# A hybrid decoder layer on one core: output weights centred by accumulating DMAs, two gate pairs ahead of the embedding, pooling operands begun one group earlier

## The chip, the cores and the metric

The kernel runs on one core of one Trainium2 chip. The metric is the time of the program on the device in microseconds (us), the median of three runs; lower is better. Engines are named as in the profile: PE (TensorE matmuls), PEld (its weight loads), DVE (VectorE), ACT (ScalarE), POOL (GpSimd), SP (the queue that issues most DMAs).

## The reference, cut to what matters

One layer on x of 1024 tokens by 2048 channels, all in float32:

```
h = x @ w_in + b_in                                   # 2048 -> 4352 columns
q, k, v, g_attn, u_pool, g_pool = split(h)
a = banded_sink_attention(q, k, v) * silu(g_attn)     # 16 heads of 64, window 128
b = multiscale_pool(u_pool, w_pool) * silu(g_pool)    # trailing means over 2/4/8/16, 4 groups
mix = concat([a, b]) @ w_out
ple = sigmoid(x @ w_gate_ple) * (p @ w_ple)
out = layer_norm(2**0.25 * x + mix + ple, gain, bias)
```

The layer norm subtracts the mean over the 2048 output channels. The kernel gets a part of that subtraction by centring rows of `w_out` beforehand: from each row of its first half (1024 input channels) the mean over the 2048 output columns is subtracted.

## The kernel before, in words

**Work on PE.** All large matmuls are cut into *jobs*: two blocks of 128 output columns by 1024 input channels by 1024 tokens. A job is done as seven block products in place of eight (a Strassen-like scheme, orders `ALONE` and `BESIDE`, lines 46 to 48). Each product is 12 matmuls of 128x128 by 128x512: weights and operands are split into a high and a low fp32r part, and three of the four combinations are multiplied (`mm3`, lines 176 to 181). A weight block is loaded as `raw`, combined on DVE (lines 215 to 218) and split by ACT into `wh` and by DVE into `wl` (`make_unit`), four products ahead of PE. Results are gathered from PSUM into `part` by ACT (`copy`) and DVE (`add`), line 346 and line 122.

**Order.** Jobs run in *groups*: a group is one job (7 products) or a pair (14 products). After each product a clock of *ticks* advances (`tick`), and work beside the matmuls is registered at a tick: `after(n, fn)` runs `fn` n ticks on; `later(n, fn)` does the same, and in addition queues what `fn` issues on PE, ACT and DVE behind the product work last marked on that engine. Instructions of SP and POOL get no such place from `later`. The order of each engine's queue is then made by the planner of the language, which takes the recorded order as priority and starts an instruction on an idle engine once its operands and buffers are free in its own estimate of time. Every queue runs strictly in that order on the chip.

**Stages** (`run`, lines 884 to 910). Five jobs of k, v, q for the first half of the input channels (s1); 25 jobs of s2: k, v, q for the second half, and everything else for the first; 20 jobs of s3: gates `gp`, pool inputs `u`, attention gates `ga` and the embedding gate `wgate` for the other half, with what follows them; s4 and s5: the output projection; s6: its last 256 tokens; the norm. The list `rest` (line 855) sets the order in s2 and s3: gp0, u0, gp1, u1, gp2, u2, gp3, u3, ga0, wgate 0 to 7, ga1, ga2, ga3. The first two and the last two jobs of a stage form pairs.

**Beside s2.** Attention runs as 16 half-heads, nine ticks apart (`heads`, called from lines 995 and 996): `begin` fetches the queries and the bias, `split` splits the queries (ACT and DVE, tick 3), `score` multiplies on PE and adds bias on DVE (tick 4 and on), `shift`, `softmax` (with an add on POOL), `share`, `trans` (PE transposes, four `affine_select` on POOL each, line 551), `value`. In the same stage `centre_weights` (line 709, called at line 999) reads the first half of `w_out` twice, in 32 cells of 256 KB each time, through the one buffer `cw`: the first pass adds up rows on DVE (line 722), the second subtracts the mean on DVE (line 122, by `tt`) and stores the cell to `wc` in DRAM.

**Beside s3.** `pool_u` makes the trailing sums of a pool block; after two blocks `mix` multiplies by `w_pool` (tick 10 after `pool_u`) and multiplies by the stored gate `sgp`, which is fetched at tick 8. `embed_in` fetches and splits p, `embed_w` the columns of `w_ple`; `embed` adds `ple` and x to each finished wgate block. They use 16 buffers `s` (`slots`) and six buffers `e` (`extras`). At the last pair of s3 these pools are closed and the same memory holds six `slots1` and eight `twos1` buffers (lines 1019 to 1024); into the latter `pooled()` fetches the pooling half of the concatenation `cc` by DMAs that ACT's queue issues (line 267). `make_pooled` splits these into the operands of s4 (`split_unit`, ACT and DVE, and four pairs of subtractions on DVE): its first two steps run at the start of the first group of s4, the next ones every two ticks. `gate_ahead` fetches the attention result `pre` for the gates.

Of the kernel before, what the change touches and what calls it, by code (L numbers as in the profile page):

```python
# [24 lines left out]
F32 = mybir.dt.float32  # L25
F32R = mybir.dt.float32r
AF = mybir.ActivationFunctionType
ALU = mybir.AluOpType
# [3 lines left out]
P = 128  # L32
T = 512
H = 4 * P
D = 2048
NB = 16
# [27 lines left out]
class Layer:  # L64
# [405 lines left out]
    def heads(self, h, j):  # L470
        nc, g = self.nc, j // 4
# [108 lines left out]
        self.later(3, split)  # L580
        for bq in range(4):
            t = 4 * (bq // 2)
            self.after(4 + 2 * bq, lambda bq=bq: score(bq))
            if bq % 2:
                self.after(8 + t, lambda bq=bq: shift(bq - 1))
                self.after(14 + t, lambda bq=bq: trans(bq - 1))
            self.after(9 + t, lambda bq=bq: softmax(bq))
            self.later(11 + t, lambda bq=bq: share(bq))
            self.after(19 + t + bq % 2, lambda bq=bq: value(bq))


    def gate_ahead(self, j):
# [15 lines left out]
    def pool_u(self, j, c):  # L608
        nc, g = self.nc, j // 2
        w = 2 << g  # L610
        out = []
        for h in range(2):
            u = self.slot()
            if h == 0:
                nc.gpsimd.memset(u[:, 0:16], 0.0)
            else:
                self.ident_act(u[:, 0:16], c[:, 0, T - 16 :], self.c(C_BIN + U0 + j))
            self.ident_act(u[:, 16:], c[:, h], self.c(C_BIN + U0 + j))
            cur, d, first = u, 1, 1
            while d < w:  # L620
                nxt = self.slot()
                end = 2 * d == w
                f = 16 if end else first
                self.tt(nxt[:, f:], cur[:, f:], cur[:, f - d : T + 16 - d], ALU.add)
                cur, d = nxt, 2 * d
                first = first + d
            if h == 0:
                self.tt(cur[:, 16 : 16 + 16], cur[:, 16 : 16 + 16], self.c(C_HEAD + 16 * g, 16), ALU.mult, nc.gpsimd)
            nc.vector.scalar_tensor_tensor(out=cur[:, 16:], in0=cur[:, 16:], scalar=1.0 / w, in1=u[:, 16:],
                                           op0=ALU.mult, op1=ALU.subtract)  # L630
            out.append(self.split(cur[:, 16:], 2 * (j % 2) + h < 3))
        self.diff[j] = out
        if j % 2:
            f = slice((g % 2) * T, (g % 2) * T + T)
            self.after(4, lambda: self.got.update({("wp", g): self.fetch(self.wpool[g // 2][:, f])}))
            self.later(8, lambda: self.got.update({("wp", g): self.split(self.got["wp", g])}))
            self.after(8, lambda: self.got.update({("sg", g): [[self.fetch(self.sgp[2 * g + e][:, h * T : h * T + T]) for e in range(2)] for h in range(2)]}))
            self.later(10, lambda: self.mix(g))

    def mix(self, g):  # L640
# [67 lines left out]

    def centre_weights(self, at, by):

        nc = self.nc
        cells = [(b, h) for b in range(NB) for h in range(2)]
        sums = self.fix.tile([P, 8, NB], F32, name="wsum")
        mean = self.fix.tile([P, 8], F32, name="wmean")
        now = []

        def fetch(b, h):
            now.append(self.load(self.tile(self.cw, [P, H], "cw"), self.wout[b, 0][:, h * H : h * H + H]))

        def add_up(b, h):  # L720
            k = now.pop().rearrange("p (k m) -> p k m", k=4)
            nc.vector.reduce_sum(sums[:, 4 * h : 4 * h + 4, b : b + 1], k, axis=mybir.AxisListType.X)

        def take_mean():
            nc.vector.reduce_sum(mean.rearrange("p (k b) -> p k b", b=1), sums, axis=mybir.AxisListType.X)
            nc.vector.tensor_scalar(out=mean, in0=mean, scalar1=1.0 / D, scalar2=None, op0=ALU.mult)

        def centre(b, h):
            w = now.pop()
            k = w.rearrange("p (k m) -> p k m", k=4)  # L730
            m = mean[:, 4 * h : 4 * h + 4].rearrange("p (k m) -> p k m", m=1).broadcast_to([P, 4, P])
            self.tt(k, k, m, ALU.subtract)
            self.load(self.wc[b, 0][:, h * H : h * H + H], w)

        for step in (add_up, centre):
            for c in cells:
                self.after(at, lambda c=c: fetch(*c))
                self.later(at + 2, lambda c=c, step=step: step(*c))
                at += by if step is centre and c[0] % 3 else 2
            if step is add_up:  # L740
                self.later(at + 1, take_mean)
                at += 2

    def mean_to_subtract(self, total, w, cut):

# [78 lines left out]
    def run(self):  # L824
# [27 lines left out]
        store = lambda w: hid if w is win else gat  # L852
        qkv = [(win, *p) for p in [(KB, VB)] + pairs(Q0, 4)]
        ga, gp, u = ([(win, *p) for p in pairs(b, 4)] for b in (GA0, GP0, U0))
        rest = [j for two in zip(gp, u) for j in two] + ga[:1] + [(wgate, *p) for p in pairs(0, 8)] + ga[1:]

        def keep(where):
            return lambda b, c: self.load(where[b], flat(c))
# [134 lines left out]
        self.after(5, lambda: build_kv(KB, self.k_build, 0))  # L993
        self.after(6, lambda: build_kv(VB, self.v_build, 0))
        for i in range(16):
            self.after(t - 1 + 9 * i, lambda i=i: self.heads(i % 2, i // 2))
        self.after(t + 63 + 8, lambda: build_kv(KB, self.k_build, 1))
        self.after(t + 63 + 22, lambda: build_kv(VB, self.v_build, 1))
        self.centre_weights(8, 3)
        begin, *steps = self.set_kept(xs[0], kept)  # L1000
        for i in range(1, n2):
            if i == n2 - 1:
# [6 lines left out]
        for i in range(n3):  # L1009
            if i == 1:  # L1010
                over.close()
                over = ExitStack()
                self.extras = self.work_pool("e2", 6, over)
            if self.groups[g + i + 1][0][0].b[0] == 0 and i < n3 - 1:
                self.after(1, self.embed_in)
                self.after(4, lambda: self.embed_w(0))
            if i == n3 - 1:

                over.close()
                work.close()  # L1020
                work = ExitStack()
                self.slot_n = T
                self.slots = self.work_pool("slots1", 6, work)
                self.twos = self.work_pool("twos1", 8, work)
                pooled()
                for n, b in enumerate(b for j in s3[-2:] for b in j.b):
                    self.after(4 + n, lambda b=b: self.gate_ahead(b - GA0))
            self.run_group(g + i, () if i else steps)
        g += n3

# [33 lines left out]
        for i in range(n4):  # L1064
            if i == 1:
                work.close()
                work = ExitStack()
                self.twos = self.work_pool("twos2", 8, work)
                p6.extend(5 * [pp] + [self.work_pool("p6", 1, work)])
                d0 = self.work_pool("d0", 4, work)  # L1070
            if i == n4 - 2:
                attended()
            self.run_group(g + i, () if i else make_pooled, renew if i == n4 - 1 else None)
        g += n4


# [134 lines left out]
```

## Time and profile before

| | |
|---|---|
| Median of 3 runs | 1505.13 us (1503.91 to 1507.74) |
| Profiled execution, its own time | 1504.51 us |
| Its span in the profile | 1502.8 us |
| Granted TensorE clock, mean | 0.99 |
| Busy: PE, DVE, ACT, POOL | 97%, 75%, 52%, 19% of the span |
| DMA: moved, mean rate | 280.38 MB, 187 GB/s |

A busy share is the time in which an instruction of that engine was in flight, over the span. Matmuls overlap each other, so PE at 97% is not a statement on its peak; what counts is where PE has no matmul in flight, and the spacing of the matmuls. Stretches of the trace are named by us from the span's start. The stages begin at these times, read as the first matmul of their first product: s2's first pair 110.8, its single jobs 148.9, its last pair 632.4; s3's first pair 676.6, single jobs 717.9, last pair 1105.3; s4's first pair 1146.8, single jobs 1190.7; s5 1305.0.

### The profile page before, as it was taken

The page shows a single profiled execution, that of the slowest core. Times are in us where ns is not written, and L with a number is a line of the kernel's source. Part 1 is how long each engine was busy: PE and PEld are TensorE (multiplying, and loading weights), DVE is VectorE, ACT ScalarE, POOL GpSimd, SP SyncE. Part 2 cuts the span into 40 slices and gives each one's busy share as a digit, 9 for nine tenths or more (in the row PEclk, how much of TensorE's full clock was granted, in tenths as well). Part 3 has the DMA queues.
Part 4 walks back from the last instruction along what each step waited for, and adds up shares of the span by engine and source line. Part 5 has one row for each costly group of instructions (what it writes and reads, how often), then busy time and mean ns, then how long its engine had stood idle before and what let it go on. Part 6 is the DMA issues. An engine that isn't in the chain of part 4 may idle for free. (4 is left out here: it accounts for less than half of the span.)

```text
span 1502.8 us, 20461 instructions
## 1 busy us (share of the span) xinstructions
PE 1453.8 (97%) x6972; PEld 1225.5 (82%) x6972; DVE 1119.7 (75%) x2030; ACT 781.1 (52%) x1550; POOL 278.9 (19%) x388
## 2 busy tenths in 40 slices
PE   8999999999999999999999998999998999999986
PEld 6788888888878888888887786888886888899985
DVE  7788678888787877888675695556558866987785
ACT  5464566666666656566633353333337433555484
POOL 0000123332333332231111111000001111111241
PEclk9999999999999999999999999999999999999998
DMA  7563875445445555557766667575768678586564
GB/s 262 202 218 101 250 208 178 140 167 174 166 168 176 174 193 180 172 182 245 189 158 175 180 155 240 160 207 160 206 189 270 150 193 236 140 239 134 153 230 143
DMA packets 101721, 280.38 MB, mean 187 GB/s; under 512 B 11632, under 2 KB 16880, under 8 KB 101616
## 3 DMA queue, kind: packets, MB, share of 16 engines
q1 hardware_dynamic: 76400, 199.89, 39.9%
q0 software_dynamic: 19712, 67.64, 19.6%
q10 hardware_dynamic: 5504, 11.54, 2.3%
q8 instruction: 55, 0.90, 0.2%
q14 instruction: 50, 0.41, 0.1%
HBM read 193.04 MB, written 85.98 MB: 186 GB/s over the span
## 5 line engine op out<-in xcount | busy, mean ns | idle before, releaser
L222 ACT CAST wh<-raw 128x512 fp32r<-128x512 f32 x428 | 264.1, 620 | 450.8 <-PE qa L180 143.2
L122 DVE TENSOR_TENSOR wl<-raw,wh 128x512 fp32r<-128x512 f32 x428 | 298.2, 702 | 141.4 <-ACT wh L222 138.5
L346 ACT COPY part<-qa 128x512 f32<-128x512 f32 (+1 forms) x180 | 103.9, 577 | 54.0 <-PE qa L181 53.0
L551 POOL TENSOR_SCALAR_AFFINE_SELECT s<-s 128x512 fp32r<-128x512 f32 x128 | 101.0, 801 | 150.5 <-ACT s L544 101.1
L122 DVE TENSOR_TENSOR part<-part,qb 128x512 f32<-128x512 f32 (+1 forms) x120 | 81.0, 675 | 50.5 <-PE qb L181 47.0
L179 PE MATMUL qa<-b11h,wh 128*128 128x512 f32 (+2 forms) x292 | 110.7, 380 | 2.0 <-ACT b11h L248 1.7
L180 PE MATMUL qa<-b11l,wh 128*128 128x512 f32 (+2 forms) x292 | 109.5, 375 | 0.2 <-DVE b11l L122 0.2
L181 PE MATMUL qa<-b11h,wl 128*128 128x512 f32 (+2 forms) x292 | 109.0, 374 | 0.4 <-DVE wl L122 0.4
L179 PE MATMUL qb<-b21h,wh 128*128 128x512 f32 (+2 forms) x292 | 109.3, 374 | 0.0
L181 PE MATMUL qb<-b21h,wl 128*128 128x512 f32 (+2 forms) x292 | 108.9, 373 | 0.0
L180 PE MATMUL qb<-b21l,wh 128*128 128x512 f32 (+2 forms) x292 | 108.7, 372 | 0.0
L179 PE MATMUL qb<-t1h,wh 128*128 128x512 f32 (+1 forms) x260 | 102.1, 393 | 4.3 <-DVE part L122 2.9
L179 PE MATMUL qa<-t2h,wh 128*128 128x512 f32 (+1 forms) x260 | 100.6, 388 | 3.5 <-ACT wh L222 3.5
L179 PE MATMUL qa<-t3h,wh 128*128 128x512 f32 (+1 forms) x260 | 100.9, 388 | 3.1 <-ACT part L346 3.1
L181 PE MATMUL qb<-t1h,wl 128*128 128x512 f32 (+1 forms) x260 | 101.1, 389 | 1.5 <-DVE wl L122 1.5
L181 PE MATMUL qa<-t2h,wl 128*128 128x512 f32 (+1 forms) x260 | 100.0, 385 | 1.5 <-DVE wl L122 1.5
L180 PE MATMUL qb<-t1l,wh 128*128 128x512 f32 (+1 forms) x260 | 100.9, 388 | 0.0
L179 PE MATMUL qa<-t4h,wh 128*128 128x512 f32 (+1 forms) x260 | 100.4, 386 | 0.3 <-DVE part L122 0.3
L179 PE MATMUL qb<-b22h,wh 128*128 128x512 f32 (+1 forms) x260 | 100.4, 386 | 0.0
L180 PE MATMUL qa<-t4l,wh 128*128 128x512 f32 (+1 forms) x260 | 99.7, 383 | 0.0
L181 PE MATMUL qa<-t4h,wl 128*128 128x512 f32 (+1 forms) x260 | 99.7, 383 | 0.0
L180 PE MATMUL qa<-t3l,wh 128*128 128x512 f32 (+1 forms) x260 | 99.7, 383 | 0.0
(286 smaller groups left out, 3568.9 us busy)
## 6 DMA issues: line engine op xcount, KB each, us to landing
raw<-in_win SPq DMA_DIRECT2D x65, 512.0 KB, 4.2
h<-part SPq DMA_DIRECT2D x34, 512.0 KB, 2.9
part<-h POOLq DMA_DIRECT2D x34, 512.0 KB, 6.0
cw<-in_wout SPq DMA_DIRECT2D x64, 256.0 KB, 3.1
raw<-in_wgate SPq DMA_DIRECT2D x32, 512.0 KB, 4.1
raw<-wc SPq DMA_DIRECT2D x32, 512.0 KB, 4.4
s<-in_x SPq DMA_DIRECT2D x44, 256.0 KB, 5.3
wc<-cw SPq DMA_DIRECT2D x32, 256.0 KB, 2.3
```

Source lines behind the costliest of these rows:

```text
L122: return (eng or self.nc.vector).tensor_tensor(out=out, in0=a, in1=b, op=op)
L179: mm(ps, wh, xh, start=start, stop=False, skip_group_check=True)
L180: mm(ps, wh, xl, start=False, stop=False, skip_group_check=True)
L181: return mm(ps, wl, xh, start=False, stop=stop, skip_group_check=True)
L222: self.unit_latest = [nc.scalar.copy(out=hi, in_=src).ins, L.lo(lo, src, hi).ins]
L346: self.mark("ACT", self.nc.scalar.copy(out=dst, in_=ps))
L551: nc.gpsimd.affine_select(out=o4, in_=a4, pattern=[[0, 4], [sign, P]], compare_op=ALU.is_ge, fill=0.0, base=0 if side else -1, channel_mul ...
```

## The change

Four things are edited.

- `centre_weights` no longer passes each cell through DVE. `w_out`'s first half is copied to `wc` by 16 DRAM-to-DRAM DMAs on SP. For each of two halves, one load and 15 accumulating DMAs issued by POOL add the 16 blocks up in the one buffer `c`; DVE reduces that sum to four values per partition and scales by -1/2048; POOL spreads them over the buffer; 16 accumulating DMAs by POOL add the buffer onto the blocks of `wc`. The steps are registered two ticks apart, from tick 14.
- In `heads`, `begin` and `split` come one tick earlier; the rest keeps its tick.
- `rest` has two attention gate jobs ahead of wgate in place of one (gp, u, ga0, ga1, wgate 0 to 7, ga2, ga3), so that the last wgate job stands directly ahead of the last pair of s3. `embed_in` and the first `embed_w` are registered four ticks later in the group ahead of wgate, and the stored gates for `mix` are fetched two ticks earlier.
- The seven steps of `make_pooled` are registered in the last group of s3, from its tick 10, two ticks apart, and no longer in s4's first group; the last four `gate_ahead` move from ticks 4 to 7 to ticks 10 to 13.

```diff
@@ heads
-            self.after(4 + 2 * bq, lambda bq=bq: score(bq))
+            self.after(5 + 2 * bq, lambda bq=bq: score(bq))
             if bq % 2:
-                self.after(8 + t, lambda bq=bq: shift(bq - 1))
-                self.after(14 + t, lambda bq=bq: trans(bq - 1))
-            self.after(9 + t, lambda bq=bq: softmax(bq))
-            self.later(11 + t, lambda bq=bq: share(bq))
-            self.after(19 + t + bq % 2, lambda bq=bq: value(bq))
+                self.after(9 + t, lambda bq=bq: shift(bq - 1))
+                self.after(15 + t, lambda bq=bq: trans(bq - 1))
+            self.after(10 + t, lambda bq=bq: softmax(bq))
+            self.later(12 + t, lambda bq=bq: share(bq))
+            self.after(20 + t + bq % 2, lambda bq=bq: value(bq))
@@ pool_u
-            self.after(8, lambda: self.got.update({("sg", g): ...
+            self.after(6, lambda: self.got.update({("sg", g): ...
@@ centre_weights: the body is replaced by
+        mean = self.fix.tile([P, 4], F32, name="wmean")
+        m4 = mean.rearrange("p (k m) -> p k m", m=1)
+
+        def steps(h):
+            f = slice(h * H, h * H + H)
+            c = self.tile(self.cw, [P, H], "cw")
+            k = c.rearrange("p (k m) -> p k m", k=4)
+
+            def take_mean():
+                nc.vector.reduce_sum(m4, k, axis=mybir.AxisListType.X)
+                nc.vector.tensor_scalar(out=mean, in0=mean, scalar1=-1.0 / D, scalar2=None, op0=ALU.mult)
+
+            def spread():
+                nc.gpsimd.tensor_copy(out=k, in_=m4.broadcast_to([P, 4, P]))
+
+            yield lambda: self.load(c, self.wout[0, 0][:, f])
+            for b in range(1, NB):
+                yield lambda b=b: nc.gpsimd.dma_start(out=c, in_=self.wout[b, 0][:, f], accum_op=ALU.add)
+            yield None
+            yield take_mean
+            yield spread
+            for b in range(NB):
+                yield lambda b=b: nc.gpsimd.dma_start(out=self.wc[b, 0][:, f], in_=c, accum_op=ALU.add)
+
+        for b in range(NB):
+            self.after(20 + 2 * b, lambda b=b: self.load(self.wc[b, 0], self.wout[b, 0]))
+        for h in range(2):
+            for step in steps(h):
+                if step:
+                    self.later(at, step)
+                at += by
@@ run
-        rest = [j for two in zip(gp, u) for j in two] + ga[:1] + [(wgate, *p) for p in pairs(0, 8)] + ga[1:]
+        rest = [j for two in zip(gp, u) for j in two] + ga[:2] + [(wgate, *p) for p in pairs(0, 8)] + ga[2:]
-            self.after(t - 1 + 9 * i, lambda i=i: self.heads(i % 2, i // 2))
+            self.after(t - 2 + 9 * i, lambda i=i: self.heads(i % 2, i // 2))
-        self.centre_weights(8, 3)
+        self.centre_weights(14, 2)
-                self.after(1, self.embed_in)
-                self.after(4, lambda: self.embed_w(0))
+                self.after(5, self.embed_in)
+                self.after(8, lambda: self.embed_w(0))
+                for n, step in enumerate(make_pooled):
+                    self.after(10 + 2 * n, step)
                 for n, b in enumerate(b for j in s3[-2:] for b in j.b):
-                    self.after(4 + n, lambda b=b: self.gate_ahead(b - GA0))
+                    self.after(10 + n, lambda b=b: self.gate_ahead(b - GA0))
-            self.run_group(g + i, () if i else make_pooled, renew if i == n4 - 1 else None)
+            self.run_group(g + i, then=renew if i == n4 - 1 else None)
```

More of the change, by code (lines that the diff above doesn't have):

```diff
@@ L636, in pool_u @@
             self.later(8, lambda: self.got.update({("wp", g): self.split(self.got["wp", g])}))
-            self.after(8, lambda: self.got.update({("sg", g): [[self.fetch(self.sgp[2 * g + e][:, h * T : h * T + T]) for e in range(2)] for h in range(2)]}))
+            self.after(6, lambda: self.got.update({("sg", g): [[self.fetch(self.sgp[2 * g + e][:, h * T : h * T + T]) for e in range(2)] for h in range(2)]}))
             self.later(10, lambda: self.mix(g))
@@ L711, in centre_weights @@
         nc = self.nc
[L712 to L742, printed above, removed]
+        mean = self.fix.tile([P, 4], F32, name="wmean")
[17 more added lines that the diff above has]
+                yield lambda b=b: nc.gpsimd.dma_start(out=self.wc[b, 0][:, f], in_=c, accum_op=ALU.add)
```

## The prediction

> **What bounds the kernel now.** First the page's busy line, then the busy time by stretches (us and instruction count of each engine, granted clock, DMA share, GB/s), their bounds being group starts.
>
> ```profile
> PE 1453.8 (97%) x6972; PEld 1225.5 (82%) x6972; DVE 1119.7 (75%) x2030; ACT 781.1 (52%) x1550; POOL 278.9 (19%) x388
> 167.90:395.00 227.10, 226.48 (x1127) 190.18 (x1126) 180.39 (x433) 140.75 (x346) 61.74 (x80) 1.00 0.56 172
> 395.00:632.40 237.40, 232.13 (x1163) 194.04 (x1161) 188.49 (x449) 146.40 (x376) 76.96 (x95) 1.00 0.53 179
> 717.90:855.10 137.20, 133.37 (x578) 107.30 (x577) 93.69 (x147) 63.88 (x109) 19.69 (x36) 1.00 0.67 179
> 893.80:932.50 38.70, 33.42 (x134) 26.81 (x133) 24.09 (x38) 15.04 (x24) 5.10 (x8) 0.91 0.78 249
> 1105.30:1146.80 41.50, 38.41 (x170) 31.45 (x168) 27.22 (x39) 21.29 (x30) 4.64 (x6) 1.00 0.83 264
> 1146.80:1190.70 43.90, 40.51 (x169) 32.52 (x168) 42.88 (x57) 23.18 (x33) 5.87 (x9) 0.96 0.53 145
> 1190.70:1266.90 76.20, 76.20 (x338) 63.06 (x337) 44.18 (x61) 26.17 (x46) 12.65 (x18) 1.00 0.78 219
> ```
>
> The last row is PE undisturbed: 28 ticks in 76.20 us, 2.72 us a tick. PE sets the end, so only what opens a hole in PE counts. The holes (length less PE busy) are 0.62, 5.27, 3.83, 5.28, 3.09 and 3.39 us, in the stretches that the change touches. Who ended them is in PE's waits over the whole run (total, times, longest):
>
> ```profile
> PE sc L179 <- ACT s L150: 5.3, 1, 5.3
> PE sc L506 <- DVE s L122: 5.2, 11, 1.2
> PE qa L179 <- ACT part L346: 3.1, 1, 3.1
> PE qb L179 <- DVE part L122: 2.9, 3, 1.0
> PE sc L179 <- DVE s L652: 2.0, 2, 1.4
> ```
>
> Row 2 is `score` waiting for `split`: it lies in the two attention stretches. Row 1 is the hole at 902 to 907 us, and the chain of work (start, length) shows its cause and its price:
>
> ```profile
> 888.86 5.64 DMA s<-in_wple
> 894.51 11.71 DMA s<-in_p
> 906.76 0.62 ACT s L150
> 907.43 0.80 PE sc L179
> 908.65 0.43 PE sc L179
> 913.75 0.24 PE qb L181
> ```
>
> The cast of `w_pool` (L150), which the last `mix` needs, stands on ACT behind casts of p that wait for a late load. Afterwards matmuls take 0.43 us until 913.75 where they otherwise take 0.23: about 15 of them, 3.0 us more.
>
> **The change part by part.**
>
> *Centring.* Its present cost, by the cell's tile; the last row is DVE's idle time for its loads:
>
> ```profile
> L136 SPq DMA_DIRECT2D cw<-in_wout x64: 327/332/1447, 31.1 to 666.7; - x64
> L722 DVE TENSOR_REDUCE wsum<-cw x32: 674/681/690, 174.2 to 377.9; 128x4 f32<-128x512 f32 x32
> L122 DVE TENSOR_TENSOR cw<-cw,wmean x32: 679/686/1229, 392.5 to 672.4; 128x512 f32<-128x512 f32 x32
> L136 SPq DMA_DIRECT2D wc<-cw x32: 319/326/327, 393.2 to 673.1; - x32
>   DMA cw<-in_wout: 11.3, 7
> ```
>
> Removed: 32 x 0.681 + 32 x 0.686 = 43.7 us of DVE, and 11.3 us of DVE standing before a load. Added on DVE: two reductions, about 1.4 us. DVE lies beside PE here, so I count none of this directly; it helps the score wait below.
>
> Traffic: removed 96 x 256 KB = 25.2 MB on SP; added 16 copies of 512 KB (8.4 MB) and two loads (0.5 MB) on SP, 62 accumulating DMAs (16.3 MB) on POOL. Priced by queue:
>
> ```profile
> q1 hardware_dynamic: 76400, 199.89, 39.9%
> q0 software_dynamic: 19712, 67.64, 19.6%
> ```
>
> That is 3.0 us of all 16 DMA engines per MB for SP's kind and 4.4 for POOL's: 75.6 us go, 26.7 + 71.7 = 98.4 come. The DMA share in some 460 us rises by 0.05 from 0.53 to 0.56: covered.
>
> The waits are the unknown. In each half the 15 accumulations write one buffer, so each waits on POOL's queue for the one before to land; behind it stand attention's adds and selects. No row shows this DMA. The nearest are:
>
> ```profile
> cw<-in_wout SPq DMA_DIRECT2D x64, 256.0 KB, 3.1
> cc<-s POOLq DMA_DIRECT2D x16, 256.0 KB, 3.8
> s<-kv POOLq DMA_DIRECT2D x8, 256.0 KB, 6.1
> part<-h POOLq DMA_DIRECT2D x34, 512.0 KB, 6.0
> L551 POOL TENSOR_SCALAR_AFFINE_SELECT s<-s x128: 628/638/1178, 215.4 to 680.9; 128x512 fp32r<-128x512 f32 x128
> L749 POOL MEMSET w<- x1: 206/206/206, 1174.8 to 1174.8; 128x128 f32 x1
> ```
>
> From 3.1 (no accumulation) to 6.1 us each; I take 5, between the POOL rows. Two ticks in this stage are 2 x 237.40/70 = 6.8 us, so at its written pace a link lands before the next is due. But POOL is not held to the written pace: the memset L749 is registered for tick 9 of s5 (after 1305 us) and ran at 1174.8, and the first cell load, registered for about 171 us, at 31.1. So the first chain, 15 x 5 = 75 us, probably runs from about 31 to 106 us, where POOL has nothing else; the second runs amid attention. There POOL is busy 61.74 + 76.96 us of 464.5; 62 more issues at the 0.9 us that such a DMA holds it add 56 us. An attention add has two ticks until `share`, a select five until `value` (6.8 and 17 us). One blocked link (5 us) is inside both. I count 0.5 us of loss, bounds 0 and 33 (worked out below).
>
> The Trainium skill (DMA: Bandwidth & Descriptors, Anatomy of one DMA) fits a POOL DMA at 2.0 us plus its bytes over 436 GB/s. By that an estimate for a link is 2.6 us, below the shortest row above, and the loss would be 0.
>
> The 16 copies have no buffer to wait for, so they too may go out near 31 us. That stretch:
>
> ```profile
> 30.00:60.00 30.00, 27.45 (x112) 21.81 (x111) 28.28 (x37) 14.53 (x23) 0.00 (x0) 0.94 0.39 139
> ```
>
> 0.61 x 30 = 18 us of the DMA engines are free, the copies need 8.4 x 3.0 = 25. They can push back the weight loads for the group at 72.7 us by at most 7 us, and those are issued from 51.6. Bounds 0 and 7; I take 0.5. The two spreads on POOL (0.64 each by L551) are nothing.
>
> *Attention one tick apart.* All score waits are at most 1.2 us, and `score` now has another 3.4 us behind `split`; what was late was `split` in a crowded DVE, which also loses 43.7 us. Next late would be `trans` and `value`, which show no wait of size. Buffers are held a tick longer for queries only. Of 0.62 + 5.27 I take **5.5 us gone**, bounds 2 and 8 (ends of matmuls are modelled, so holes may be larger than shown).
>
> *Two gate pairs ahead.* u3's `mix` falls two groups before the first embedding result is needed, and p is fetched 11 ticks later against it: its casts no longer stand ahead of `w_pool`'s. The hole of 5.28 us and the 3.0 us of slow matmuls go. What is late next is p itself: cast at tick 14 of ga1's group, needed at tick 19 at the earliest, 5 ticks or 13.6 us, against a landing of 11.7 us at worst above. I take **8 us gone**, bounds 0 and 8.3.
>
> *Stored gates two ticks earlier.* Of the 3.83 us, 2.0 wait for L652, which multiplies by the loaded gate. I take **1.5**, bounds -1 (four buffers held longer) and 3.8.
>
> *Pooling operands earlier.* Row 7 shows DVE 42.88 of 43.90 us busy while PE loses 3.39 us: the splits and subtractions fall together with the last gates. Begun four ticks earlier, the first splits and subtractions precede these gates. The clock of 0.96 there costs 0.04 x 43.9 = 1.8 us more. Against it: the last wgate job now finishes inside this pair, and the fetches need memory which its additions use until tick 8; ACT issues them. The hole of 3.09 us before was such a wait:
>
> ```profile
> ACT wh L222 <- DMA two<-cc: 7.0, 1, 7.0
> ```
>
> The later `gate_ahead` takes four to six loads off that burst. Of 3.09 + 3.39 + 1.8 = 8.3 I take **5 gone**, bounds -8 and 8.3.
>
> The Trainium skill (TensorE: Matmul & The Clock Gate, Part 1) lowers the clock after an idle window of about 3.4 us. No single wait in row 7's stretch is that long, yet its clock is 0.96, so the trace doesn't bear the rule out there. By it alone the 1.8 us is not this hole's and the term would be at most 6.5.
>
> **Sum**, against the profiled execution's own 1504.5 us: -5.5 - 8 - 1.5 - 5 + 0.5 + 0.5 = -19.0, so 1485.5. The median of the runs is 0.6 above that execution: **1486 us**.
>
> **Rivals.**
>
> - *POOL's chain takes over; slower.* If the planner sets the second half's 15 links at the 3.1 us of a plain load and they land at the 6.3 us of accumulating ones (the median of all L359 DMAs is below), POOL falls 15 x 3.2 = 48 us behind attention; 17 us are slack, 31 to 33 are lost: 1486 + 32 = **1518**. It decides from a lag over 17 us on: a planned pace below 5.1 us. For it: POOL runs ahead of its ticks. Against: attention's work between links spaces them.
>
> ```profile
> DMA to landing us min/median/max: 4.5/6.3/13.3
> ```
>
> - *The start pays:* copies ahead of the weight loads at 51.6 us, up to 7 us: **1492**.
> - *The transition doesn't gain:* ACT waits for memory until tick 8, PE loses as much as before and some 4 more: 1486 + 5 + 4 = **1495**.
> - *The embedding stall stays,* as the change does not do what it says: SP stood up to 22.3 us before a weight buffer ahead of p, and the order of SP's queue is the planner's. 1486 + 8 = **1494**.
>
> ```profile
> SPq L136 <- DVE wl L122: 49.2, 6, 22.3
> ```
>
> - *Two of these at once,* or a chain lag just over the slack: about **1503**.
>
> **How the numbers follow.** Forecast (1478 to 1491) 0.44, start 0.11, transition 0.14, stall 0.08, two at once 0.11, chain 0.12. A measurement of this kernel can tell 0.3%, 4.5 us, from no change. Faster: 0.44 + 0.11 + 0.14 + 0.08 = 0.77; same: 0.11; slower: 0.12. The range reaches down to all the holes gone (0.62 + 5.27 + 3.83 + 8.3 + 8.3 = 26, to 1479, and 2 more for modelled ends: 1477) and up to two rivals at once, 1503; the chain and some edges, 2 in 10, are out.
>
> **What would show it.** In the changed kernel: no wait of sc L506 over 0.3 us; no matmul at 0.43 us near the first wgate group; DVE below 0.75 busy in the attention stretch; the split of b11 for s4 well before the last gates. Wrong if PE waits for POOL's selects or ACT for `share`, if raw loads land after 72 us, or if ACT's wait for `two<-cc` remains.

## The result, and the profile after

| | before | changed kernel |
|---|---|---|
| Median of 4 runs each | 1504.65 us (1503.91 to 1507.74) | 1555.18 us (1549.9 to 1556.6) |
| Ratio, 95% interval | | 1.0325 (1.0297 to 1.0354) |
| Profiled execution, its own time | 1504.51 us | 1549.9 us |
| Span, granted clock | 1502.8 us, 0.989 | 1547.7 us, 0.975 |

The change makes the kernel slower by 50 us; 1486 us was predicted, with a range that ended at 1503. The profiled execution is the fastest of its four. First the page of the changed kernel: the busy line and the two queues.

```profile
PE 1467.5 (95%) x6972; PEld 1235.3 (80%) x6972; DVE 1092.0 (71%) x1968; ACT 782.7 (51%) x1550; POOL 326.5 (21%) x452
...
q1 hardware_dynamic: 63376, 183.63, 34.7%
q0 software_dynamic: 28640, 83.90, 25.4%
```

PE has the same 6972 matmuls. DVE lost 62 instructions and 28 us of busy time, POOL gained 64 and 48 us. The bookkeeping of the change came out as expected; the order in which things wait did not. To see where, I split the span at the same group starts in both kernels. A stretch's **loss** is worked out as its length less the sum of its matmuls, each at the median spacing of its kind in the trace (a single job without attention is 84 matmuls in 19.0 us, and loses nothing). The level of a loss depends on which matmuls are counted as one kind (in attention by some 7 us, in every kernel alike); the differences between kernels hardly do.

| Stretch (its bounds before; in the changed kernel) | loss before | loss after | predicted change |
|---|---|---|---|
| start (0 to 148.9; to 153.4) | 11.1 | 15.6 | +0.5 |
| attention (to 676.6; to 716.4) | 20.7 | 56.2 | -5.5 and +0.5 |
| seven groups with `mix` (to 855.1; to 892.0) | 8.5 | 5.6 | -1.5 |
| gates and embedding (to 1105.3; to 1132.2) | 11.6 | 7.0 | -8 |
| passage: last pair of s3, first of s4 (to 1190.7; to 1235.9) | 9.5 | 22.3 | -5 |
| rest | 12.7 | 12.2 | 0 |

The losses add up to 74.1 and 118.9 us, 44.8 apart, as the spans are (44.9). Two places make the result: attention, 35 us worse, and the passage, 13 us worse. The windows of the changed kernel over its attention stretch (length; busy time and count of each engine; granted clock, DMA share, GB/s):

```profile
153.40:328.00 174.60, 174.60 (x853) 146.45 (x852) 116.55 (x273) 103.99 (x243) 52.32 (x69) 1.00 0.62 170
328.00:435.00 107.00, 84.09 (x360) 67.13 (x359) 63.37 (x140) 45.75 (x116) 42.61 (x52) 0.86 0.57 132
435.00:573.50 138.50, 137.53 (x694) 116.04 (x694) 103.01 (x259) 89.70 (x230) 46.05 (x63) 1.00 0.37 131
573.50:602.00 28.50, 24.97 (x121) 20.64 (x120) 19.95 (x47) 13.52 (x33) 16.07 (x19) 0.95 1.03 234
```

Nearly all of the attention loss lies in rows 2 and 4: PE is idle for 22.9 us of 107 and the matmuls that it has run at a clock of 0.86. In rows 1 and 3 PE is idle for 1 us in 313: there the later ticks of attention work. What POOL did, and who waited, in row 2 (the engine's timeline, with its idle time and releaser; then the waits: total, times, longest):

```profile
337.02 4.24 POOL L551 TENSOR_SCALAR_AFFINE_SELECT s<-s 128x512 fp32r<-128x512 f32 x4
345.39 0.90 POOL L730 DMA_DIRECT2D cw<-in_wout  x1 [4.12 <-DMA cw<-in_wout]
345.99 1.07 POOL L122 TENSOR_TENSOR s<-s 128x256 f32<-128x256 f32 x1
351.86 0.89 POOL L730 DMA_DIRECT2D cw<-in_wout  x1 [4.80 <-DMA cw<-in_wout]
357.38 0.87 POOL L730 DMA_DIRECT2D cw<-in_wout  x1 [4.63 <-DMA cw<-in_wout]
357.95 1.05 POOL L122 TENSOR_TENSOR s<-s 128x256 f32<-128x256 f32 x1
361.46 0.88 POOL L730 DMA_DIRECT2D cw<-in_wout  x1 [2.46 <-DMA cw<-in_wout]
```

```profile
POOL cw L730 <- DMA cw<-in_wout: 41.9, 14, 4.8
ACT s L535 <- POOL s L122: 33.6, 5, 9.4
...
PE sc L506 <- DVE s L122: 8.4, 4, 5.8
...
PE qb L179 <- ACT part L346: 6.7, 1, 6.7
```

POOL's queue runs in order. From 345.4 to 408.3 us the second half's 15 links of the accumulating chain (L730) go out; the first half's had gone from 36.5 to 134.2, ahead of attention. Ahead of each attention add (L122) or group of four selects (L551) stand one to three links, and most links wait 2.5 to 4.8 us for the one before to land. ACT, which needs the adds for `share` (L535), stands still for 33.6 us in five waits, 9.4 us in the longest. Behind `share` on ACT stand the casts of weights and the evictions of PSUM, and those PE does feel: the evictions in the last row, and the score wait by way of DVE.

The passage, by the waits of the changed kernel and by ACT's timeline:

```profile
ACT part L346 <- DMA two<-cc: 13.6, 1, 13.6
...
PE qa L179 <- ACT part L346: 8.5, 2, 5.6
PE qb L179 <- ACT wh L222: 8.5, 1, 8.5
```

```profile
1156.14 0.58 ACT L346 COPY part<-qa 128x512 f32<-128x512 f32 x1
1156.50 13.79 ACTq L267 DMA_DIRECT2D two<-cc  x8
1170.33 0.59 ACT L346 COPY part<-qa 128x512 f32<-128x512 f32 x1 [13.61 <-DMA two<-cc]
```

ACT issues the eight fetches of the pooling operands itself. From 1156.5 to 1170.3 its sequencer is held by them. PE waits 5.6 us, until 1171.0, for the eviction of PSUM behind them, and 2.9 us more for an eviction at the start of s4 (until 1187.4). The last row is another hole: PE waits for a weight's cast from 1198.8 to 1207.3, in the first pair of s4, 28 us after the last fetch has left ACT.

### The profile page after: what moved, and what is told of

Same layout as the page of the kernel before. It is cut to its first block, busy times and chain, and to the rows that moved or that the text cites. A ratio compares the mean times of both kernels' runs of the same rounds, so it can differ in the third digit from the quotient of the medians.

```text
span 1547.7 us, 20393 instructions
## 1 busy us (share of the span) xinstructions
PE 1467.5 (95%) x6972; PEld 1235.3 (80%) x6972; DVE 1092.0 (71%) x1968; ACT 782.7 (51%) x1550; POOL 326.5 (21%) x452
## 5 line engine op out<-in xcount | busy, mean ns | idle before, releaser
L122 DVE TENSOR_TENSOR wl<-raw,wh 128x512 fp32r<-128x512 f32 x428 | 301.6, 708 | 182.9 <-ACT wh L222 172.3
L346 ACT COPY part<-qa 128x512 f32<-128x512 f32 (+1 forms) x180 | 103.9, 577 | 56.9 <-PE qa L181 39.4
L551 POOL TENSOR_SCALAR_AFFINE_SELECT s<-s 128x512 fp32r<-128x512 f32 x128 | 99.4, 821 | 124.5 <-ACT s L544 90.0
L122 DVE TENSOR_TENSOR part<-part,qb 128x512 f32<-128x512 f32 (+1 forms) x120 | 81.0, 675 | 58.6 <-PE qb L181 54.4
L181 PE MATMUL qa<-t3h,wl 128*128 128x512 f32 (+1 forms) x260 | 101.0, 389 | 1.5 <-DVE wl L122 1.5
L180 PE MATMUL qb<-b22l,wh 128*128 128x512 f32 (+1 forms) x260 | 100.6, 387 | 0.0
```

What stands on the lines that cost most here:

```text
L122: return (eng or self.nc.vector).tensor_tensor(out=out, in0=a, in1=b, op=op)
L180: mm(ps, wh, xl, start=False, stop=False, skip_group_check=True)
L181: return mm(ps, wl, xh, start=False, stop=stop, skip_group_check=True)
L346: self.mark("ACT", self.nc.scalar.copy(out=dst, in_=ps))
L551: nc.gpsimd.affine_select(out=o4, in_=a4, pattern=[[0, 4], [sign, P]], compare_op=ALU.is_ge, fill=0.0, base=0 if side else -1, channel_mul ...
```

## The experiments

Each kernel was timed beside the kernel before; the ratio to it is given with its 95% interval. The last two columns are the losses in attention and in the passage, as above.

| Run | What it is | median us | ratio (interval) | attention | passage |
|---|---|---|---|---|---|
| e1 | changed kernel, old centring | 1509.36 | 1.0031 (1.0018 to 1.0043) | 17.2 | 23.4 |
| e2 | changed kernel, centring behind attention on POOL ("pinned") | 1507.37 | 1.0028 (1.0016 to 1.0041) | 16.2 | 22.4 |
| e3 | e2, the 16 copies behind the weight loads | 1508.35 | 1.0021 (1.0006 to 1.0037) | 19.2 | 23.5 |
| e4 | changed kernel, everything after attention as before | 1538.85 | 1.0228 (1.0206 to 1.0250) | 57.1 | 7.0 |
| e5 | e4, pinned | 1492.73 | 0.9929 (0.9902 to 0.9957) | 14.3 | 6.3 |
| e6 | e5 with the pooling begun early | 1498.80 | 0.9958 (0.9944 to 0.9972) | 13.7 | 13.5 |
| e7 | e5 with the new gate order | 1505.80 | 1.0011 (0.9996 to 1.0025) | 14.7 | 21.3 |
| e8 | e5 with the embedding begun later | 1498.07 | 0.9953 (0.9929 to 0.9978) | 13.6 | 9.6 |
| e9 | attention's ticks and the stored gates alone | 1495.46 | 0.9927 (0.9907 to 0.9946) | 18.1 | 6.5 |
| e10 | e4, centring steps four ticks apart | 1553.75 | 1.0304 (1.0261 to 1.0346) | 53.8 | 10.6 |
| e11 | e6, the last stored gates early again | 1500.35 | 0.9959 (0.9941 to 0.9976) | 15.4 | 12.0 |
| e12 | e4, only the writes pinned | 1522.53 | 1.0114 (1.0097 to 1.0131) | 40.9 | 6.3 |
| e13 | e4, only the links pinned | 1509.63 | 1.0034 (1.0021 to 1.0047) | 32.1 | 4.8 |

### Is it the centring, and is it its place in POOL's queue? (e1 to e3)

e1 puts the body of `centre_weights` of before back.

```diff
-        self.centre_weights(14, 2)    # and its body
+        self.centre_weights(8, 3)     # and the body of before
```

> The changed kernel with the centring of before put back; all other edits kept. Theory: the changed kernel lost its time in three places. By the spacing of PE's matmuls against the undisturbed spacing, PE lost some 40 us beyond the background in attention (328 to 435 and 574 to 602 us), where POOL's queue holds a serial chain of accumulating DMAs ahead of attention's adds and selects; 4 to 5 us at the start, where 16 copies stand ahead of weight loads; and 13 us more than before at the passage from the gates to the output projection. So this run is expected at 1555 - 40 - 4.5 = about 1510 us, with the passage as bad as in the changed kernel. Rival (traffic or the order of the gates is the cause, not the centring): above 1540 us.

46 us go, and attention's loss falls to 17.2: the centring is the whole of the attention loss. It stays 0.3% slower than before, so the rest of the change has a loss of its own, in the passage (23.4).

Why POOL ran ahead of its ticks can be read in the code. A step that is registered with `later` isn't placed ahead of the last marked instruction of each engine:

```
    def later(self, n, fn):
        ...
                for ins in self.latest.values():
                    ctx.enter_context(self.tc.issue_after(ins))
```

Marks are set on work of PE, ACT and DVE alone (L346, L348, L397, L427). Nothing on POOL is marked, so POOL's queue can take the links long before attention's adds and selects of the same tick. e2 marks these:

```diff
-                self.tt(cur, old, cur, ALU.add, nc.gpsimd)
+                self.mark("POOL", self.tt(cur, old, cur, ALU.add, nc.gpsimd))
...
-                    nc.gpsimd.affine_select(out=o4, in_=a4, ...)
+                    self.mark("POOL", nc.gpsimd.affine_select(out=o4, in_=a4, ...))
```

> The changed kernel, but POOL's adds and selects of attention are marked, so that each step of the centring is queued on POOL behind the attention work recorded by its tick, and no longer as early as the planner finds POOL idle. Same DMAs, same bytes, same count; the copies on SP stay where they are. Theory (place in POOL's queue): the 40 us in attention go, about 1515 us. Rival (the accumulating DMAs cost as such, by traffic or by holding POOL 0.9 us each): the time stays above 1540 us and PE's waits for POOL stay.

48 us go with every DMA of the new centring still there. So it is not what the DMAs carry in all, but where they stand and how closely they come. e3 adds a pin for the 16 copies:

```diff
-            self.load(t, job.w[job.b[i], job.half])
+            self.mark("SP", self.nc.sync.dma_start(out=t, in_=job.w[job.b[i], job.half]))
...
-            self.after(20 + 2 * b, lambda b=b: self.load(self.wc[b, 0], self.wout[b, 0]))
+            self.later(20 + 2 * b, lambda b=b: self.load(self.wc[b, 0], self.wout[b, 0]))
```

> As the one with POOL's steps pinned, and the 16 copies (and the two loads) on SP are queued behind the weight loads recorded by their tick. Theory: the start goes back to the spacing of before (group at 72.7 us, not 75.4; 4 to 5 us less in all), about 1510 us. Rival: the start is slower for another reason, no change against the run with POOL alone pinned.

No gain. In the profiled executions the start loses 10.6 to 15.7 us where the copies go out early, 13.2 in e3 and 11.0 to 12.7 with the old centring (before, e1, e9). The 4.5 us of the changed kernel's start lie inside that scatter; whether the copies have a part in it stays open.

### Links or writes? (e10, e12, e13)

The prediction rested on the written pace. e10 doubles it, on the kernel of e4 (whose expectation stands in the next part):

```diff
-        self.centre_weights(14, 2)
+        self.centre_weights(14, 4)
```

> As e4 (changed centring unpinned, everything after attention as before; 1538.9), but the centring's steps are registered four ticks apart in place of two. If the written pace holds the links apart (13 us between two of them, three times their landing), attention loses little: 1495 to 1505. If the recorder queues POOL's steps as early as it can whatever their tick, and what counts is how many links stand ahead of attention's adds and selects, the loss moves to later groups and stays of the same size: 1530 to 1545.

The pace helps nothing. The attention loss stays, 53.8 against 57.1, and the second half's writes now come from 906 us on, in the stretch of gates and embedding, which loses 27.4 us against e4's 11.3. By the tile's rows of this run the last links go at 518.6 us and the last writes at 942.8:

```profile
L735 POOL DMA_DIRECT2D wc<-cw x32: 857/873/1664, 413.4 to 942.8; - x32
L730 POOL DMA_DIRECT2D cw<-in_wout x30: 857/874/1064, 35.2 to 518.6; - x30
```

e12 and e13 pin one kind of DMA alone. In e12 each write is issued after the last add or select that is noted by then, in e13 each link:

```diff
+                def write(b=b):
+                    with self.tc.issue_after(self.noted):
+                        nc.gpsimd.dma_start(out=self.wc[b, 0][:, f], in_=c, accum_op=ALU.add)
+                yield write
-                yield lambda b=b: nc.gpsimd.dma_start(out=self.wc[b, 0][:, f], in_=c, accum_op=ALU.add)
```

> As e4 (changed centring unpinned, everything after attention as before; 1538.9 against 1492.7 with the whole centring pinned, so 46 us), but only the 32 writes to the weights are put behind attention's adds and selects; the 30 links stay where the recorder puts them. If the 46 us are the links alone (each waits for the one before to land, with adds and selects behind it), nearly all stay: 1530 to 1540. If the writes have a share (16 of them hold POOL's queue from 305.7 to 337 us in the changed kernel), their share goes: 1505 to 1525.

> The mirror of e12: only the links are put behind attention's adds and selects, the writes stay where the recorder puts them. If the links are the cost: 1493 to 1500. If the writes have a share: that share of the 46 us stays, 1505 to 1525. If the sum of what e12 and e13 save is far from 46 us, the two act on each other.

With neither kind in the way (e5) the time is 1492.7, with both (e4) 1538.9. The links alone cost 1522.5 - 1492.7 = **29.8 us**, the writes alone 1509.6 - 1492.7 = **16.9 us**; together 46.7, against 46.1 measured with both. Within the scatter of these runs the two add up.

How writes that wait for nothing of each other can cost PE shows in e13. POOL's timeline, DVE's timeline, the waits and the windows around the first write burst (line numbers of this kernel are 4 to 7 higher):

```profile
318.12 0.86 POOL L742 DMA_DIRECT2D wc<-cw  x1 [1.39 <-issue]
321.20 0.88 POOL L742 DMA_DIRECT2D wc<-cw  x1 [2.21 <-issue]
322.32 0.88 POOL L742 DMA_DIRECT2D wc<-cw  x1 [0.24 <-issue]
322.89 1.07 POOL L122 TENSOR_TENSOR s<-s 128x256 f32<-128x256 f32 x1
```

```profile
316.44 0.69 DVE L122 TENSOR_TENSOR part<-part,qa 128x512 f32<-128x512 f32 x1 [0.93 <-PE qa L185]
325.24 0.69 DVE L122 TENSOR_TENSOR wl<-raw,wh 128x512 fp32r<-128x512 f32 x1 [8.10 <-ACT wh L226]
```

```profile
POOL wc L742 <- issue: 14.5, 11, 2.9
ACT s L539 <- POOL s L122: 8.6, 1, 8.6
DVE wl L122 <- ACT wh L226: 8.5, 2, 8.1
...
PE sc L510 <- DVE s L122: 5.6, 1, 5.6
```

```profile
299.00:323.00 24.00, 24.00 (x123) 20.18 (x123) 16.00 (x36) 10.65 (x28) 12.49 (x17) 1.00 1.01 221
323.00:333.00 10.00, 4.45 (x21) 3.60 (x19) 7.57 (x17) 6.66 (x18) 5.90 (x8) 0.76 1.03 147
```

Read it from the top. The add at 322.89 stands behind the writes, which leave POOL about 2 us apart although each holds it 0.86 us. ACT waits 8.6 us for that add with `share` at the head of its queue; the cast of a weight stands behind, so DVE waits 8.1 us for the cast; the queries' split stands behind on DVE, so PE waits 5.6 us. Four in-order queues pass one delay on. The DMA share is 1.01 and 1.03 of 16 engines during the burst, so the DMA engines are full too; which of the two, POOL or the full DMA engines, sets the pitch of the writes was not separated.

### What is the rest worth? (e4, e5, e9)

e4 undoes the change after attention: the gate order, the embedding's ticks, the pooling's and the last `gate_ahead`s'.

```diff
-        rest = ... + ga[:2] + [(wgate, *p) for p in pairs(0, 8)] + ga[2:]
+        rest = ... + ga[:1] + [(wgate, *p) for p in pairs(0, 8)] + ga[1:]
...
-                self.after(5, self.embed_in)
-                self.after(8, lambda: self.embed_w(0))
+                self.after(1, self.embed_in)
+                self.after(4, lambda: self.embed_w(0))
...
-                for n, step in enumerate(make_pooled):
-                    self.after(10 + 2 * n, step)
...
-                    self.after(10 + n, lambda b=b: self.gate_ahead(b - GA0))
+                    self.after(4 + n, lambda b=b: self.gate_ahead(b - GA0))
...
-            self.run_group(g + i, then=renew if i == n4 - 1 else None)
+            self.run_group(g + i, () if i else make_pooled, renew if i == n4 - 1 else None)
```

> The changed kernel with the order of gates and embedding, the fetches of p, the pooling steps and the late gate fetches as before; the new centring and the earlier query split stay. Theory: the passage to the output projection loses 9.5 us of PE as before and not 22 (minus 13), the embedding stall comes back (plus 5): about 1547 us, with the attention loss unchanged. Rival (the passage is late only because everything before it is late): about 1555 to 1560 us.

16 us less than the changed kernel: the passage's loss falls from 22.3 to 7.0, and only 4.3 come back in the embedding (7.0 to 11.3). e5 is e4 with the pin of e2:

> The changed kernel with the centring's POOL steps put behind attention's adds and selects in POOL's queue, and with the gate order, the embedding's ticks and the pooling's ticks of before. Against the pinned kernel alone (1507.4): if the passage from s3 to s4 is what eats the gain of the attention ticks, 22 us of loss there go back to about 10 and the embedding's 4 us go back to 9: 1507 - 12 + 5 = 1500, and by the undoing that was measured without the pin (-16) 1491. Expected 1495, faster than before by 9. Rival: the loss in the passage comes with the new centring or the attention ticks, not with the order and the pooling: 1507 or more.

12 us below the kernel before. Its wait rows over attention show the mechanism:

```profile
POOL s L122 <- ACT s L522: 88.4, 34, 6.2
POOL s L551 <- ACT s L544: 77.0, 23, 6.8
POOL cw L730 <- DMA cw<-in_wout: 55.0, 15, 5.9
```

POOL waits for links as long as ever, 55.0 us against 41.9. But now its adds wait for ACT and not ACT for its adds: the row of ACT waiting for POOL's add, 33.6 us in the changed kernel, is not among the 40 longest here. The same waiting costs PE nothing when nothing urgent stands behind it. The pin spreads the links as well: in e5 all but the first go out amid attention, 14 from 195 to 282 us and 15 from 427 to 518, so that attention holds nearly twice as many links as in the changed kernel, and does not suffer.

e9 keeps of the change only attention's ticks and the stored gates' fetch (the edits of e4, with the old centring):

> Of the change only attention's later ticks and the stored gates' earlier fetch are left; centring, gate order, embedding and pooling are those of before. Theory A (the ticks alone remove the score waits): the attention stretches lose the 9 us that they lost less in e5, so 1492 to 1495. Theory B (DVE must also lose the 44 us of centring for the score waits to go): 1498 to 1502, and waits of score for split remain in the trace.

It comes to 0.9927, the same as e5 by the intervals. So the new centring, even where it does no harm, shows no gain of its own, although DVE is busy for 30 us less in attention (386.4 against 416.5); a gain of a few us, as the attention losses of the two profiles differ (14.3 and 18.1), isn't excluded. Of what e9 gains over the kernel before, its profile has 2.6 us in attention, some 3 in the groups with `mix` and 3.0 in the passage, where nothing was edited.

### The passage (e6, e7, e8, e11)

All four start from e5. e6 keeps the early pooling steps and the late `gate_ahead` of the change, with gate order and embedding as before; e7 keeps the change's gate order and embedding, with the pooling as before; e8 keeps only the embedding's later ticks.

> As e5, but with the pooling operands begun early as in the change; only the order of the gate pairs and the embedding's ticks are those of before. Theory A (the order is the cost: wg7's additions fall into the last pair of s3 and hold the memory that the pooling's fetches need): the fetches go out near tick 10 without a wait and the operands are ready, so the passage falls below before's 10 us to some 6: 1491. Theory B (the early pooling work itself is the cost: it shares DVE and ACT with the last gates): the passage stays near 22 us and the time near 1507 + 5 = 1512.

> As e5, but with two gate pairs ahead of the embedding and its later ticks as in the change; only the pooling operands and the stored gates are those of before. Theory A (the order is the cost): the passage still loses 20 us or more, 1505 to 1512. Theory B (the early pooling is the cost): the passage falls back to about 10 us and the embedding's stall stays shorter: 1507 - 12 = 1495.

> As e5, with one edit of the change kept: the embedding's first fetches and casts at ticks 5 and 8 of the group ahead in place of 1 and 4, in the gate order of before. If the stall at the first embedding group is only that p's casts stand on ACT ahead of w_pool's, four ticks (11 us) are enough to let w_pool's cast by, and 4 us or more of the 9 us go without the second gate pair: 4 to 8 us below e5, some 1489. If p is then late itself, or the place of the last mix is what matters: the same as e5 within 2 us.

Against e5's 1492.7, the new order with the embedding's later ticks costs 13.1 us (e7) and the early pooling alone 6.1 (e6), both together 14.6 (e2, 1507.4). Theory A named the larger part; B has a part too. PE's waits keep the two apart: e7 has the waits for evictions, behind ACT's fetches and at the start of s4 (4.5 and 3.8 us), and none over 1.5 us for a cast, e6 the wait for a cast in the first pair of s4 (9.1 us) and 1.9 us for an eviction, and the changed kernel has both. e8 is 5.3 us slower than e5. In the profiles 4.3 us of that lie in its start (15.7 us lost there against 11.4), where nothing was edited, and 3.3 in its passage (9.6 against 6.3); its embedding loses 9.3 against 10.1. So the embedding's ticks alone gain at most 1 us where they should, and whether they cost anything elsewhere isn't shown.

In e7 the same burst stands on ACT as in the changed kernel, though the pooling was not touched (ACT's timeline):

```profile
1111.80 0.58 ACT L346 COPY part<-qa 128x512 f32<-128x512 f32 x1
1112.15 12.67 ACTq L267 DMA_DIRECT2D two<-cc  x8
1124.87 0.59 ACT L346 COPY part<-qa 128x512 f32<-128x512 f32 x1 [12.49 <-DMA two<-cc]
```

and DVE's timeline gives a reason for its late start: the last embedding additions (L691) of the eighth wgate pair, whose memory the fetches take over. The second fetch leaves at 1114.3, as the last of them ends.

```profile
1109.43 0.69 DVE L691 SCALAR_TENSOR_TENSOR part<-s,part 128x512 f32<-128x512 f32 x1
...
1113.57 0.69 DVE L691 SCALAR_TENSOR_TENSOR part<-s,part 128x512 f32<-128x512 f32 x1
```

That is 25.7 us after the pair's start at 1087.9. With the old order the last addition comes at 1095.9, 1.6 us after the start at 1094.3 (e5). In e5 the eight fetches leave ACT from 1105.2 to 1114.1 us, and its longest wait for them in the passage is 4.3 us. What holds the later fetches of e7, up to 1124.2, isn't the additions; by the trace three of them wait for loads of `pre` or for an earlier fetch. This was not tested.

e6's loss is another. Here are the windows of the first pair of s4 in e6 and, below, in e5:

```profile
1135.20:1184.30 49.10, 39.97 (x169) 32.64 (x168) 43.09 (x57) 23.07 (x33) 6.07 (x10) 0.90 0.54 147
```

```profile
1132.40:1176.60 44.20, 40.76 (x170) 32.55 (x169) 42.86 (x57) 23.20 (x33) 5.90 (x9) 0.96 0.53 145
```

DVE has the same 57 instructions and 43 us of work in that pair: beginning the steps earlier took none of it out. It only changed the order, and in e6 PE has a wait of 9.1 us for one cast while DVE is busy. That cast waits for a weight block that DVE combines at 1153.9 us, behind two subtractions of the pooling (2.35 us) and four multiplications of the gates (2.49 us). e11 asks whether the late gates are to blame:

```diff
-                    self.after(10 + n, lambda b=b: self.gate_ahead(b - GA0))
+                    self.after(4 + n, lambda b=b: self.gate_ahead(b - GA0))
```

> As e6 (old gate order, pooling operands begun early and the last stored gates fetched late; 1498.8), but the stored gates fetched at ticks 4 to 7 as before. If the 9 us hole of e6 at 1146 us comes from the late gates (their loads, then DVE's multiplications, stand ahead of the split weights), it goes and the early operands pay: 1488 to 1492. If the early splits on DVE themselves are the cost, the time stays within 2 us of e6: 1497 to 1501.

They are not: 1500.4, as e6, with a loss of 12.0. The early steps are the cost. Which of DVE's instructions would have to move was not tried.

## Why the prediction was wrong

- **POOL's chain, +0.5 with bounds 0 and 33; measured 46.** This step failed. The words are "One blocked link (5 us) is inside both" slacks. The size of a link was not the fault: 5 us were taken, and amid attention a link of the changed kernel lands after 3.7 us in the median and the next follows 4.1 us after it. The number of links was wrong: the queue has one to three ahead of each add or group of selects, and the delay is paid again at each. The links' 29.8 us lie inside the bounds. The writes' 16.9 us had no term: they were counted as traffic, "covered" by the average over 460 us, while 16 of them come within some 32 us.
- **The rival of POOL's chain** (1518, a chance of 0.12) had the engine and the wait right, and its 31 to 33 us look like the links' 29.8. That is partly luck: its rule, with the planned pace of 3.1 us that it assumed and the measured 4.1, gives 15 x 1.0 = 15 us of lag, inside its own slack of 17.
- **Its signs.** Two of the signs that it named for being wrong came: ACT waits for the adds of `share` (33.6 us), and its wait for `two<-cc` remains (13.6 us).
- **Its reason.** The prediction had the right row against itself, that POOL runs ahead of its written ticks (L749), and then set "attention's work between links spaces them" against the rival. e10 shows that the pace written down decides nothing. The slack was also read off POOL and the consumers' ticks; but `share` stands in ACT's queue as early as the planner likes, and a late add stops ACT with everything behind it.
- **A price from the Trainium skill.** DMA: Bandwidth & Descriptors, Anatomy of one DMA, gave an estimate of 2.6 us for a link. The trace does not agree: 3.7 us in the median for the links amid attention, 6.8 for those of the start.
- **Attention's ticks, -5.5 with bounds 2 and 8: right.** The attention loss falls by 6.4 in e5, where DVE is relieved too as the prediction had it, and by 2.6 in e9, where it is not; the score wait is 0.6 us in e9 in place of 5.2. In the changed kernel it was hidden under the chain, where score waits of 8.4 us stand again, as the delayed splits of the chain above.
- **Stored gates, -1.5: right**, with 2.9 us measured (8.5 to 5.6 in the `mix` groups, and the same in e5 and e9), and the wait for L652 is gone.
- **Two gate pairs ahead, -8: wrong in balance.** The embedding's stretch gained 4.6 us, of which p's stall is a part. What was late next was not p but the passage: the eighth wgate pair now ends inside the last pair of s3, as the prediction says itself in the term of the pooling. The order with the embedding's ticks costs 13.1 us net in e7.
- **Pooling earlier, -5 with bounds -8 and 8.3: wrong sign**, 6.1 us lost in e6. The step that failed is that "the first splits and subtractions precede these gates": the DVE work stayed in the pair. The first splits were early already. In the kernel before, the cast of b11 runs 13 us ahead of the group at whose start it is registered (1146.8):

  ```profile
  L248 ACT CAST b11h<-two x2: 1043/1044/1045, 1133.7 to 1134.6; 128x1024 fp32r<-128x1024 f32 x2
  ```

  With the early steps (e6) it runs 27.2 us after the start of the last pair of s3, without them (e5) 25.0.
- **The rival on the transition had a part of the mechanism** (ACT waits for memory until tick 8), and put its price over the kernel before at 4 us; 12.8 were lost. The late cast in the first pair of s4 (8.5 us) was not in that price.
- **The start, +0.5:** 4.5 in one profile, inside the scatter of the others.
- **The embedding's stall:** partly gone; PE's wait for the cast of `w_pool` (L150), 5.3 us before, is 2.1.

Without the chain the sum would still have failed: e2 has no loss from it and stands at 1507.4, where the prediction less its 0.5 would be 1485.5. So two errors of mechanism stand apart, 46 us on POOL and 22 between e2 and the forecast, nearly all in the passage and the embedding.

## What to carry to other kernels

Before an engine with an in-order queue is given a chain of dependent DMAs, count how many links can stand ahead of each urgent instruction there, and follow the delay through every in-order queue behind it; free time on that engine says nothing. Where a planner sets the order, find out what binds it: a step without an ordering edge on its own engine isn't held by its tick. A step that is moved earlier pays only if the busiest engine's work really leaves the crowded stretch, and if the memory that it fetches into is free by then.

If one edit is to be kept, it is attention's later ticks with the earlier stored gates: 0.9927 (0.9907 to 0.9946) by themselves, about 10 us below the kernel before, and by the intervals no run was faster.

## What was not expected of the hardware

- A link of the accumulating chain (256 KB, from POOL) took longer where the DMA engines were fuller. Amid attention (345 to 409 us, DMA share 0.57) it lands after 3.7 us in the median and the next follows 4.1 us after it, less than the 6.1 us that plain DMAs of that size took before (`s<-kv`). At the start (share 0.96 from 36 to 110 us) it is 6.8 and 7.2. The medians over the whole changed kernel, in us from issue to landing:

```profile
wc<-in_wout SPq DMA_DIRECT2D x16, 512.0 KB, 7.5
wc<-cw POOLq DMA_DIRECT2D x32, 256.0 KB, 5.7
cw<-in_wout POOLq DMA_DIRECT2D x30, 256.0 KB, 4.4
```

- Sixteen accumulating writes in a row and what goes beside them fill the DMA engines (share 1.01 over 24 us in e13) at only 221 GB/s; from 36 to 110 us of the changed kernel a share of 0.96 goes with 324 GB/s.
- With PE's 5.6 us wait in e13 (326.1 to 331.6 us) the clock falls to 0.76 in the 10 us window that holds most of it. In windows of 2 us it is 0.50 from 330 to 338 us: it falls within the wait and stays low for over 6 us after it, in which matmuls start 0.43 us apart in place of 0.23. So a hole is paid twice, as the changed kernel's 0.86 between 328 and 435 us shows over a longer stretch. The Trainium skill (TensorE: Matmul & The Clock Gate, Part 1) lowers the clock after an idle window of about 3.4 us; this wait is longer, and the trace agrees.
